# Attention heads in pairs at every second step, and the second mixer's gate factors one step earlier

## The chip, the cores and the metric

The kernel runs on one core of a Trainium2 chip. Its time is the device time of one execution in microseconds (us); the time of a kernel is the median of its runs. The engines of the core work side by side, each through its own queue in program order: TensorE (PE; weight loads are shown as PEld) multiplies and transposes, VectorE (DVE), ScalarE (ACT) and GpSimd (POOL) work on elements, and SyncE (SP) issues nearly all DMA transfers.

## The reference

One layer of a hybrid block for a sequence of 256 positions of width 1024, all in float32:

```python
ada = c @ w_ada + b_ada                       # shift, scale, gate
h = _rmsnorm(x, norm_w) * (1 + scale) + shift
(qa, ka, va, za, qm, km, vm, zm, om, ig, fg, ga, gm) = jnp.split(h @ w_in, SPLIT_IDX, axis=-1)
qa, ka = _rmsnorm(heads(qa)), _rmsnorm(heads(ka))
ya = merge(_moba_attention(qa, ka, heads(va), rel_bias))    # 8 heads of 128, causal, with a bias by distance
ya = (ya * silu(za)) @ w_att_proj
qm, km = jnp.split(silu(_causal_dwconv(concat(qm, km), conv_w, conv_b)), 2, axis=-1)
hm = _mlstm_chunkwise(qm, km * 256 ** -0.5, vm, ig + b_igate, fg + b_fgate)   # 4 heads of 256
ym = (rmsnorm(sigmoid(om) * hm) * silu(zm)) @ w_ml_proj
return x + gate * ((sigmoid(ga) * ya + sigmoid(gm) * ym) @ w_out)
```

With 256 positions there is a single block of attention, so the attention of one head is an ordinary causal softmax of 256 by 256. The second mixer (mLSTM) is computed here for the whole sequence at once, with factors made from the running sum and the running maximum of its two gates.

## The kernel before

**Precision.** Every large product is done in three matmuls: each float32 operand is split into a high part and a low part (ACT makes the high part `wh` of a weight tile, L448; DVE, or POOL for a few, the low part `wl`, L452), and high by high, low by high and high by low are summed in PSUM. The products of attention, scores and values, are plain float32 matmuls, which the trace shows as two records each. Transposes are matmuls against an identity.

**First stage.** The norm, the modulation and the products for q and k of attention run first, under a step list of their own (to about 55 us). The change doesn't touch it.

**The loop.** The rest is a list of chunks, each one half or one third of a weight matrix's columns: va (three chunks), za, qm, km, att (the projection after attention), zm, vm, om, ga, gm, ml and out (two chunks each). Each chunk is four steps `g`, and a step is the products with two blocks of 128 rows of the weight: 12 matmuls with 344 columns in the chunks of va (steps 0 to 11), 24 matmuls with 256 columns in za, qm, km and att (steps 12 to 43), 12 matmuls with 512 columns in zm, vm and om. `done(name, half)` is the first step after a chunk: 16 for the first half of za, 20 for its second.

**Order within a step.** In program order a step `g` (L950) does this: it splits the weights of step `g + 4` (`split`, L441): first `wh` on ACT, then the callbacks registered with `between(g, ...)`, then `wl` on DVE. When a chunk ends it takes its result out of PSUM. Then come the callbacks registered with `at(g, ...)`, then weight loads for buffers that came free (`pump`, L934, onto SP's queue), and last the step's own matmuls. Each engine executes its share in that order and waits where data are missing. Five buffers of `wh` and `wl` and six of raw weights are in use.

**Attention, by head `h`** (A0 is 10):

- `att_qk` (L599): two products give the scores, without the masked quarter, in one PSUM buffer `aux`; two DVE reductions add the bias, negate, and leave the row's extreme in `st`. P has 4 buffers.
- `att_exp` (L614): two exponents on ACT, with their sums. It is an `at` callback of step 10 + h.
- `att_norm` (L620): DVE takes the reciprocal of the sums and scales P, in two parts. At step 11 + h, ahead of the scores of the next head.
- `att_PT` (L626): three transposes of P on TensorE into one `aux` buffer, and a copy on ACT. At step 13 + h, ahead of all else that step has between.
- `att_av` (L634): for two heads, the product with the values (four matmuls), the product with silu(za) on DVE, and its split into `yah` (ACT) and `yal` (POOL). At steps 18, 20, 21 and 22 for heads 0, 2, 4 and 6 and the one after each.

`aux` (L431) is a ring of four PSUM buffers that all these share, the transposes of q and k (`qk_T`, at steps 7, 8, 10 and 12) and of the gates too.

**The second mixer's gates.** `gates_0` to `gates_7` (L518 on) work on a few rows of 256 values. `gates_4` (step 15) makes the running sum and maximum by DVE scans. `gates_5` (L561, step 17) takes the negative maximum and the sum of both on DVE, the exponent `GE` on ACT, and writes the negative maximum to memory (`md`, a DMA of SP). `gates_6` (step 18) reads it back spread over all partitions (`NM`, a DMA of SP). `gates_T` (L584, step 18) transposes `GE` on TensorE. `gates_7` (19) and `gates_D` (21) make the decay factors from NM.

Of the kernel before, what the change touches and what calls it, by code (L numbers as in the profile page):

```python
# [18 lines left out]
AH, AD = 8, 128  # L19
# [47 lines left out]
def tile_hybrid(ctx: ExitStack, tc: tile.TileContext, x, c, params2, w_row, w_va, ada_mod, ada_gate,  # L67
# [117 lines left out]
    def split_low(k, e, c0, c1):  # L185
        h, l = wsp[k]
        cs = slice(c0, c1)
        e.tensor_tensor(l[:, cs], wrow[k][:, cs], h[:, cs].bitcast(F32), op=OP.subtract)  # L188
# [44 lines left out]
    for j in range(4):  # L233
        n, q = divmod(j, 2)
# [68 lines left out]
    for step in P1_STEPS:  # L303
# [3 lines left out]
        else:  # L307
# [5 lines left out]
                 h=lambda k: split_low(k, nc.vector, 1536, NR), G=modulate_low,  # L313
# [35 lines left out]
    def done(name, half):  # L349
        return 4 * (C[name, half] + 1)  # L350
# [104 lines left out]
    hooks, hooks_between = {}, {}  # L455

    def at(step, fn, *a):
        hooks.setdefault(step, []).append((fn, a))

    def between(step, fn, *a):  # L460
        hooks_between.setdefault(step, []).append((fn, a))
# [45 lines left out]
    f = slice(32, 36)  # L507
# [375 lines left out]
    at(10, gates_2)  # L883
    at(12, qk_T, "k", 1)
    A0 = 10
    for h in range(AH):
        between(A0 + 1 + h, att_norm, h)
        between(A0 + h, att_qk, h)
        hooks_between.setdefault(A0 + 3 + h, []).insert(0, (att_PT, (h,)))
        at(A0 + h, att_exp, h)  # L890
    for step, fn in ((12, gates_3), (14, gates_copy), (15, gates_4), (17, gates_5), (18, gates_6), (18, gates_T),
                     (19, gates_7), (21, gates_D)):
        at(step, fn)
    for nm in ("qm", "km"):
# [3 lines left out]
                at(s + q, lambda i, *a: conv(mmt[i], *a), C[nm, hf], hf, nm, q)  # L898
                at(s + q + 1, conv_silu, hf, nm, q)
    for q in range(2):  # L900
        at(done("za", 0) + 2 + 2 * q, att_av, 2 * q)
        at(done("za", 1) + 1 + q, att_av, 4 + 2 * q)
    s = 4 * C["zm", 0]
    for half in range(2):
        at(s + 5 * half, ml_split, half)
# [170 lines left out]
```

## Time and profile before

| | |
|---|---|
| median of 3 runs | 351.48 us (351.43 to 351.65) |
| profiled execution, its own time | 351.84 us |
| its span, first to last instruction | 350.0 us |
| mean granted TensorE clock | 1.000 |
| PE busy | 344.3 us (98%) |
| DVE busy | 247.0 us (71%) |
| ACT busy | 213.3 us (61%) |
| POOL busy | 87.8 us (25%) |

Rows of a timeline give the start and the length of an instruction in us, the engine, the line in the kernel, the operation, what it writes and reads, shapes and a count; in brackets stands how long the engine was idle before it and what ended that. Matmuls are pipelined and their recorded ends are modelled, so their records overlap: what a matmul costs in a stream is the distance between two starts, not the length of its record. Rows of waits give who waited for whom, us in total, times, and the longest. Rows of stretches of time give the busy time of PE, PEld, DVE, ACT and POOL, each with its count, then the granted clock, the share of the DMA engines and GB/s.

### The profile page before, as it was taken

The page shows a single profiled execution, that of the slowest core. Times are in us where ns is not written, and L with a number is a line of the kernel's source. Part 1 is how long each engine was busy: PE and PEld are TensorE (multiplying, and loading weights), DVE is VectorE, ACT ScalarE, POOL GpSimd, SP SyncE. Part 2 cuts the span into 40 slices and gives each one's busy share as a digit, 9 for nine tenths or more (in the row PEclk, how much of TensorE's full clock was granted, in tenths as well). Part 3 has the DMA queues.
Part 4 walks back from the last instruction along what each step waited for, and adds up shares of the span by engine and source line. Part 5 has one row for each costly group of instructions (what it writes and reads, how often), then busy time and mean ns, then how long its engine had stood idle before and what let it go on. Part 6 is the DMA issues. An engine that isn't in the chain of part 4 may idle for free.

```text
span 350.0 us, 6175 instructions
## 1 busy us (share of the span) xinstructions
PE 344.3 (98%) x2432; PEld 323.1 (92%) x2432; DVE 247.0 (71%) x369; ACT 213.3 (61%) x331; POOL 87.8 (25%) x81
## 2 busy tenths in 40 slices
PE   8999999999999999999999999999999999999996
PEld 7788889999999999999998888888899999999995
DVE  4999996976994437768866693864475775469961
ACT  4768779799777867675646554445646374543510
POOL 4400002942202462555004352000010320452000
PEclk9999999999999999999999999999999999999999
DMA  7999999890671554493874837659119129291011
GB/s 286 416 413 416 415 419 418 223 385 13 197 285 62 161 200 134 151 375 125 322 279 151 330 120 245 237 163 388 51 29 381 72 70 367 107 292 69 2 62 60
DMA packets 23517, 77.79 MB, mean 222 GB/s; under 512 B 3001, under 2 KB 4929, under 8 KB 22849
## 3 DMA queue, kind: packets, MB, share of 16 engines
q1 hardware_dynamic: 23336, 76.87, 59.9%
q10 hardware_dynamic: 152, 0.53, 0.5%
q8 instruction: 19, 0.31, 0.3%
q14 instruction: 10, 0.07, 0.1%
HBM read 76.14 MB, written 1.25 MB: 221 GB/s over the span
## 4 chain that ended last, share of the span: by engine, by line
PE 96%; DMA 2%; DVE 1%; issue 0%; SPq 0%; ACT 0%; DVEq 0%; ACTq 0%
PE mm L1009 15%; PE mm L1006 15%; PE mm L1008 15%; PE pm L198 13%; PE mm L999 8%; PE mm L1000 8%; PE mm L1001 8%; PE mm L992 3%; DMA adat<-in_ada_mod_dram 2%; PE mm L1021 1%; PE aux L642 1%; PE mm L1020 1%; PE mm L1019 1%; PE aux L492 1%; PE aux L604 1%; PE aux L762 1%
## 5 line engine op out<-in xcount | busy, mean ns | idle before, releaser
L452 DVE TENSOR_TENSOR wl<-raw,wh 128x1024 fp32r<-128x1024 f32 (+1 forms) x92 | 118.7, 1302 | 64.1 <-ACT wh L448 64.1
L448 ACT CAST wh<-raw 128x1024 fp32r<-128x1024 f32 (+1 forms) x100 | 100.5, 1015 | 54.2 <-PE mm L1001 26.7
L1006 PE MATMUL mm<-hTh,wh 128*128 128x256 f32 x320 | 90.0, 281 | 0.0
L1008 PE MATMUL mm<-hTl,wh 128*128 128x256 f32 x320 | 88.7, 277 | 0.0
L1009 PE MATMUL mm<-hTh,wl 128*128 128x256 f32 x320 | 88.7, 277 | 0.0
L1006 PEld LDWEIGHTS mm<-hTh,wh 128*128 128x128 f32 x320 | 60.2, 188 | 0.0
L1008 PEld LDWEIGHTS mm<-hTl,wh 128*128 128x128 f32 x320 | 60.2, 188 | 0.0
L1009 PEld LDWEIGHTS mm<-hTh,wl 128*128 128x128 f32 x320 | 60.1, 188 | 0.0
L999 PE MATMUL mm<-wh,hTh 128*128 128x512 f32 (+1 forms) x144 | 53.0, 368 | 0.0
L1000 PE MATMUL mm<-wl,hTh 128*128 128x512 f32 (+1 forms) x144 | 52.6, 365 | 0.0
L1001 PE MATMUL mm<-wh,hTl 128*128 128x512 f32 (+1 forms) x144 | 52.6, 365 | 0.0
L1001 PEld LDWEIGHTS mm<-wh,hTl 128*128 128x128 f32 x144 | 27.0, 188 | 3.8
L999 PEld LDWEIGHTS mm<-wh,hTh 128*128 128x128 f32 x144 | 27.0, 188 | 3.6
L1000 PEld LDWEIGHTS mm<-wl,hTh 128*128 128x128 f32 x144 | 27.1, 188 | 3.5
L452 POOL TENSOR_TENSOR wl<-raw,wh 128x1024 fp32r<-128x1024 f32 x8 | 19.5, 2461 | 18.4 <-ACT wh L448 12.1
L183 ACT CAST wrh<-raw 128x512 fp32r<-128x512 f32 (+1 forms) x24 | 18.2, 761 | 8.0 <-DMA raw<-in_w_row_dram 7.9
L188 DVE TENSOR_TENSOR wrl<-raw,wrh 128x512 fp32r<-128x512 f32 (+1 forms) x26 | 20.3, 807 | 0.5 <-ACT wrh L183 0.5
L198 PE MATMUL pm<-wrh,hTh 128*128 128x512 f32 x64 | 19.9, 392 | 0.8 <-ACT hTh L168 0.8
L198 PE MATMUL pm<-wrh,hTl 128*128 128x512 f32 x64 | 19.8, 391 | 0.0
L198 PE MATMUL pm<-wrl,hTh 128*128 128x512 f32 x64 | 18.7, 391 | 0.0
L1009 PE MATMUL mm<-yah,wl 128*128 128x256 f32 x64 | 17.7, 276 | 0.0
L1006 PE MATMUL mm<-yah,wh 128*128 128x256 f32 x64 | 17.7, 276 | 0.0
(218 smaller groups left out, 659.3 us busy)
## 6 DMA issues: line engine op xcount, KB each, us to landing
raw<-in_w_in_dram SPq DMA_DIRECT2D x32, 1024.0 KB, 5.2
adat<-in_ada_mod_dram SPq DMA_DIRECT2D x16, 512.0 KB, 8.8
raw<-in_w_va_dram SPq DMA_DIRECT2D x6, 688.0 KB, 9.2
raw<-in_ada_gate_dram SPq DMA_DIRECT2D x4, 1024.0 KB, 6.8
raw<-in_w_att_proj_dram SPq DMA_DIRECT2D x4, 1024.0 KB, 4.8
raw<-in_w_ml_proj_dram SPq DMA_DIRECT2D x4, 1024.0 KB, 6.3
raw<-in_w_out_dram SPq DMA_DIRECT2D x4, 1024.0 KB, 6.3
raw<-in_w_row_dram SPq DMA_DIRECT2D x15, 256.0 KB, 8.1
```

Source lines behind the costliest of these rows:

```text
L183: copy(wsp[k][0][:, c0:c1], wrow[k][:, c0:c1])
L188: e.tensor_tensor(l[:, cs], wrow[k][:, cs], h[:, cs].bitcast(F32), op=OP.subtract)
L198: nc.tensor.matmul(pm[ch][:, t], a[:, k, t * 128:(t + 1) * 128], b[:, cs], start=k == 0 and i == 0, stop=k == KT - 1 and i == 2)
L448: nc.scalar.copy(h, w)
L452: e.tensor_tensor(l, w, h.bitcast(F32), op=OP.subtract)
L992: nc.tensor.matmul(mmt[ci][:, t, cs], a, w[:, kk, cs], start=first and i == 0 and c0 == 0 and w is wh, stop=last and i == 1 and c0 > 0, sk ...
L999: nc.tensor.matmul(o, a, wh[:, kk], start=first, stop=False)
L1000: nc.tensor.matmul(o, a, wl[:, kk], start=False, stop=False)
L1001: nc.tensor.matmul(o, b, wh[:, kk], start=False, stop=last)
L1006: nc.tensor.matmul(o, wh[:, kk, cs], sh_[:, k], start=first and i % 2 == 0, stop=False, skip_group_check=True)
L1008: nc.tensor.matmul(o, wh[:, kk, cs], sl_[:, k], start=False, stop=False, skip_group_check=True)
L1009: nc.tensor.matmul(o, wl[:, kk, cs], sh_[:, k], start=False, stop=last and i % 2 == 1, skip_group_check=True)
```

## The change

The callbacks of attention are registered for pairs of heads (h, h + 1) with h = 0, 2, 4, 6. Scores and exponents of both heads come at step 10 + h, the normalisation of both at step 11 + h, the transposes of both P at step 14 + h. So scores stand at steps 10, 12, 14 and 16, normalisation at 11, 13, 15 and 17, transposes at 14, 16, 18 and 20. Within a step the order is transposes, scores; the sort at the end of the new lines puts transposes first. The products with the values come for heads 0 to 3 at step 20 and for heads 4 to 7 at step 22. `gates_5` goes from step 17 to step 16. The functions that are called are not changed, nor is the number of their instructions.

```diff
     A0 = 10
-    for h in range(AH):
-        between(A0 + 1 + h, att_norm, h)
-        between(A0 + h, att_qk, h)
-        hooks_between.setdefault(A0 + 3 + h, []).insert(0, (att_PT, (h,)))
-        at(A0 + h, att_exp, h)
-    for step, fn in ((12, gates_3), (14, gates_copy), (15, gates_4), (17, gates_5), (18, gates_6), (18, gates_T),
+    for h in range(0, AH, 2):
+        for fn, d in ((att_PT, 4), (att_qk, 0), (att_norm, 1)):
+            for hh in (h, h + 1):
+                between(A0 + h + d, fn, hh)
+        for hh in (h, h + 1):
+            at(A0 + h, att_exp, hh)
+    for i in range(A0 + 4, A0 + AH + 4, 2):
+        hooks_between[i].sort(key=lambda f: f[0] is not att_PT)
+    for step, fn in ((12, gates_3), (14, gates_copy), (15, gates_4), (16, gates_5), (18, gates_6), (18, gates_T),
                      (19, gates_7), (21, gates_D)):
         at(step, fn)
...
     for q in range(2):
-        at(done("za", 0) + 2 + 2 * q, att_av, 2 * q)
-        at(done("za", 1) + 1 + q, att_av, 4 + 2 * q)
+        at(done("za", 1), att_av, 2 * q)
+        at(done("za", 1) + 2, att_av, 4 + 2 * q)
```

## The prediction

> **What bounds the kernel now.** I read the page first: the busy line and the chain of work that ended last, then who waited for whom on the matmul queue.
>
> ```profile
> PE 344.3 (98%) x2432; PEld 323.1 (92%) x2432; DVE 247.0 (71%) x369; ACT 213.3 (61%) x331; POOL 87.8 (25%) x81
> PE 96%; DMA 2%; DVE 1%; issue 0%; SPq 0%; ACT 0%; DVEq 0%; ACTq 0%
> PE pm L198 <- ACT hTh L168: 0.8, 1, 0.8
> ```
>
> TensorE is busy for 344.3 of 350.0 us and holds 96% of the chain; its last own wait of the whole run, 0.8 us, is in the first stage, at 11 us. So moving work of another engine gains nothing here by itself. Only three things can change the time: a TensorE wait inside the stage touched, TensorE's cost of going from one kind of matmul to another, and the pace of its stream. The stage is steps 10 to 22 of the loop, from about 76 us (L605 at 76.59 below) to 122.83. Its waits, weight loads included, hold one line for TensorE, and it is the gates':
>
> ```profile
> PEld aux L587 <- ACT GE L565: 0.2, 1, 0.2
> ```
>
> **Part 1, the gate factors one step sooner.** The timeline around step 18, DVE, ACT and PE:
>
> ```profile
> 101.81 0.16 DVE L622 RECIPROCAL st<-st 128x2 f32<-128x2 f32 x1
> 102.65 0.42 DVE L608 CUSTOM_DVE_ANT_0 P<-aux,Tb 128x256 f32<-128x256 f32 x1
> 103.21 1.22 DVE L452 TENSOR_TENSOR wl<-raw,wh 128x1024 fp32r<-128x1024 f32 x1
> 104.55 0.41 DVE L564 TENSOR_TENSOR G<-G 4x256 f32<-4x256 f32 x1
> 105.05 0.42 ACT L565 ACTIVATE GE<-G 4x256 f32<-4x256 f32 x1 [0.89 <-DVE st L622]
> 105.42 0.27 PE L631 MATMUL aux<-ident,P 128*128 128x128 f32 x1
> 105.62 0.31 PE L587 MATMUL aux<-ident,GE 36*128 36x36 f32 x2
> 105.86 0.70 PE L642 MATMUL aux<-PT,vat 128*128 128x256 f32 x2
> 106.40 0.38 PE L644 MATMUL aux<-PT,vat 128*128 128x128 f32 x2
> 106.62 0.60 PE L642 MATMUL aux<-PT,vat 128*128 128x256 f32 x2
> 107.05 0.38 PE L644 MATMUL aux<-PT,vat 128*128 128x128 f32 x2
> ```
>
> The GE factors are ready at 105.05 + 0.42 = 105.47; TensorE transposes them (L587) at 105.62. From the last transpose of P to it go 0.20 us where 0.11 is usual (94.00 to 94.33 for three, below), and the first L642 takes 0.54 to the next instruction where the second takes 0.43. That is 0.09 + 0.11 = 0.20 us, the size of the wait.
>
> With gates_5 at step 16, DVE no longer has ahead of it the normalisation of head 6 (101.81 to 102.65, at most 0.84) and the split for step 21 (1.22): about 2.0 us sooner, so GE is ready at about 103.5. On ACT the exponent of head 7 now stands before it, but its input is sooner too, since head 7 moves to step 16. TensorE asks at about 105.3, so the cover is some 1.8 us. **Gain 0.20**, bounds 0 (if DVE runs 1.8 us late) and 0.20. No new DVE, ACT or table load is issued. The step also issues a DMA, the write of md, and moves it past one step of SyncE's queue:
>
> ```profile
> 66.22 31.91 SPq L376 DMA_DIRECT2D raw<-in_w_in_dram  x8
> 104.65 0.32 SPq L567 DMA_DIRECT2D md<-G  x1
> 105.92 0.38 SPq L573 DMA_DIRECT2D NM<-md  x1
> 116.03 4.36 SPq L376 DMA_DIRECT2D raw<-in_w_in_dram  x2
> ```
>
> The eight weight loads before it are issued by 98.13 at the latest, from steps that lie before 16, and the next load comes at 116.03, after NM. Nothing is queued behind the waiting write but NM's read, which stays at step 18. Cost 0; if a load did stand behind it, it would lose the 2 us of earlier DVE work at most, against the lead shown in part 3.
>
> **Part 2, fewer changes between the two kinds of work.** Before, TensorE leaves its stream for attention at each of the steps 10 to 22: 13 blocks. After, scores come at 10, 12, 14 and 16, transposes of P at 14, 16, 18 and 20, values at 20 and 22, and the transposes of q, k and gates at 10, 12 and 18: 7 blocks. The matmuls in them are the same. So what a block costs beyond its matmuls counts six times:
>
> ```profile
> 76.59 0.38 PE L605 MATMUL aux<-kT,qT 128*128 128x128 f32 x2
> 76.81 1.04 PE L492 MATMUL aux<-ident,qt 128*128 128x128 f32 x8
> 94.00 0.27 PE L629 MATMUL aux<-ident,P 128*128 128x128 f32 x1
> 94.33 0.60 PE L604 MATMUL aux<-kT,qT 128*128 128x256 f32 x2
> 94.76 0.38 PE L605 MATMUL aux<-kT,qT 128*128 128x128 f32 x2
> 97.74 0.27 PE L629 MATMUL aux<-ident,P 128*128 128x128 f32 x1
> 110.02 0.27 PE L629 MATMUL aux<-ident,P 128*128 128x128 f32 x1
> 113.09 0.27 PE L629 MATMUL aux<-ident,P 128*128 128x128 f32 x1
> 122.83 0.36 PE L1006 MATMUL mm<-hTh,wh 128*128 128x256 f32 x1
> 182.77 0.40 PE L999 MATMUL mm<-wh,hTh 128*128 128x512 f32 x1
> ```
>
> The undisturbed stream is 22 steps of 24 matmuls from 122.83 to 182.77: 59.94 / 528 = 0.1135 us each, 2.72 a step. A step with a head takes 97.74 - 94.00 = 3.74. Taken off: 2.72, three transposes 0.33, L604 0.43, L605 0.22 (its distance to the next instruction inside a block, 76.59 to 76.81). What is left is 0.04; for transposes alone 3.07 - 2.72 - 0.33 = 0.02. I take 0.03 for steps 11, 13, 15 and 17 and 0.02 for 19 and 21: **gain 0.16**, bounds 0 and 0.24 (six times 0.04).
>
> **Part 3, what moves and stays hidden.** Scores of odd heads one step sooner, transposes of even heads one step later, values of heads 0 and 1 two steps later. The reduction that takes the scores waits for TensorE at the head of DVE's queue, and behind it stands the split of the weights four steps on. Its lead covers that:
>
> ```profile
> 108.78 1.22 DVE L452 TENSOR_TENSOR wl<-raw,wh 128x1024 fp32r<-128x1024 f32 x1 [3.16 <-ACT wh L448]
> ```
>
> This is the split for step 22, done at 110.00, used at 122.83: 12.8 us of lead, among the latest of the stage. A pair puts one head's reduction (102.65 to 103.21, 0.56) more ahead of it in an even step, and one head's normalisation (0.84) more in an odd one; on ACT one more exponent. All of it is under 3 us, so cost 0; without the lead it would be about a microsecond. The four score buffers in PSUM come round each two steps (7.5 us), the four P buffers too, and a buffer's transposes stand ahead of its next scores on TensorE. Values at 20 need transposed heads 0 to 3 copied at 14 and 16; their results are first used at step 36. Cost 0 each, nothing below 0 since TensorE waits for none of them today. The sort of the callbacks puts transposes first, where they already are.
>
> **Part 4, the pace, which the trace shows and does not explain.** Stretches between blocks run at one of two paces and mostly keep theirs to the next block. First and last rows of four stretches:
>
> ```profile
> 83.76 0.28 PE L1008 MATMUL mm<-hTl,wh 128*128 128x256 f32 x1
> 86.35 0.28 PE L1009 MATMUL mm<-hTh,wl 128*128 128x256 f32 x1
> 91.39 0.28 PE L1008 MATMUL mm<-hTl,wh 128*128 128x256 f32 x1
> 93.89 0.28 PE L1009 MATMUL mm<-hTh,wl 128*128 128x256 f32 x1
> 114.84 0.28 PE L1008 MATMUL mm<-hTl,wh 128*128 128x256 f32 x1
> 117.44 0.28 PE L1009 MATMUL mm<-hTh,wl 128*128 128x256 f32 x1
> 269.27 0.28 PE L1008 MATMUL mm<-hTl,wh 128*128 128x256 f32 x1
> 277.51 0.28 PE L1009 MATMUL mm<-hTh,wl 128*128 128x256 f32 x1
> ```
>
> 22 distances each in the first three: 0.1177, 0.1136, 0.1182; 70 in the fourth: 0.1177. A slow step costs 24 x 0.0042 = 0.10. Slow are steps 12 (first pair) and 20 (third), 13 by the same reading, and 10 and 11 with 12 matmuls each at half the price: 0.40 in the stage. Every block draws anew, the change alters every block, so this term is open: -0.40 if all turn quick, +0.70 if the seven others (14 to 19, 21) turn slow. I take 0, the same share as now, since nothing in the identical blocks says which pace follows (step 13 slow, step 14 quick, after the same instructions).
>
> **Sum.** -0.20 - 0.16 + 0 = -0.36. Against the profiled execution's own 351.84 (span 350.0 and 1.84 around it) that is 351.48; that execution lies 0.36 above the median of the runs, 351.48, and from the median the forecast is **351.12**. A measurement of this kernel tells a difference from about 0.2%, 0.70 us: below 350.78 or above 352.18. So I forecast no change that shows.
>
> **Rivals.**
>
> *The stream after step 22 goes slow.* The block that ends at 122.83 is followed by 528 matmuls with no further block. Now they are quick, after a block of one pair of heads; then it is a block of two pairs. If that stretch draws the slow pace and keeps it: 528 x 0.0042 = +2.2, 351.12 + 2.2 = 353.3. It shows as slower from 1.06 / 0.0042 = 252 slow matmuls on. For it: 72 matmuls at 269 us stayed slow throughout. Against: no stretch longer than those was slow. 0.08.
>
> *All short stretches turn quick.* 351.12 - 0.40 = 350.7. For it: steps 14 to 19 are almost all quick, and half as many draws. 0.20.
>
> *The short stretches turn slow instead,* half of the bound, +0.35 to +0.70: 351.5 to 351.8. For it: steps 10 to 13 are slow one after another. 0.12.
>
> *The earlier gates do nothing,* because DVE, which runs its stage without pause, gets to them late: 351.32. Against: 1.8 us of cover. 0.08.
>
> *The clock drops in the larger blocks.* If transposes and short matmuls of step 20 (two heads transposed 0.65, two pairs of values 2.6: 3.25 us) took twice their time on a lowered clock, and the next 24 matmuls too, that would be +3.25 and +2.72 at most; I take one step's, +2.7, so 353.8. The rows against it:
>
> ```profile
> L492 PE MATMUL aux<-ident,qt x8: 272/272/273, 76.8 to 77.6; 128*128 128x128 f32 x8
> 76.20:90.30 14.10, 14.10 (x109) 13.89 (x108) 10.27 (x26) 13.32 (x26) 5.24 (x6) 1.00 0.30 104
> ```
>
> Eight transposes in a row left the granted clock at 1.00 in that stretch. 0.02. The Trainium skill's TensorE: Matmul & The Clock Gate, Part 4: PE-mode transpose, states that the transpose mode does not count as busy work for the clock gate in the same way, at about 275 ns a transpose. By that rule grouping six transposes would speak against this change; the trace has the duration, 272 ns, but shows no lower clock behind them, and six are fewer than these eight.
>
> **Chances and range.** The forecast's own case 0.50, the rivals 0.20, 0.12, 0.08, 0.08 and 0.02. Faster by over 0.2% takes most of the quick rival and a little of the forecast, where later stretches (269 us, 0.30) turn quick as well: 0.22. Slower takes the long stretch, the clock and a little of the slow rival: 0.11. Within: 0.67. The range goes from 350.5 (both gains, all short stretches quick, some of the later ones) to 352.0 (no gain kept, most of the slow bound); the long stretch lies outside.
>
> **What would show it.** Right: no wait of L587 for GE, GE ready by 104 us; seven blocks, the stretches between them 48 matmuls long; step 22's block starting about 0.3 us sooner, but for the paces; TensorE with no new wait; the time from there to the end unchanged. Wrong: a wait of a matmul for wl, PT or an aux buffer between steps 14 and 24; a pace over 0.117 after step 22; a granted clock below 1.00.

## The result, and the profile after

The changed kernel is slower: 354.21 us median (353.84 to 354.51) against 351.46 us for the kernel before (351.32 to 351.65), a ratio of 1.0078 with a 95% interval of 1.0062 to 1.0094. The forecast was 351.12 us, 350.5 to 352.0, so the time lies outside the range. The rival that had 0.08, "the stream after step 22 goes slow" at 353.3 us, is what the trace shows.

In the kernel after, lines from L892 on stand three further down; the matmuls of the 256-column chunks are L1009, L1011 and L1012. In the kernels of the experiments that have lines added they stand further down still. The page of the kernel after, its busy line and its chain:

```profile
span 352.0 us, 6176 instructions
PE 346.6 (98%) x2432; PEld 325.1 (92%) x2432; DVE 246.8 (70%) x369; ACT 213.1 (61%) x331; POOL 90.6 (26%) x81
PE 97%; DMA 1%; ACT 0%; DVE 0%; SPq 0%; issue 0%
```

The span grew by 2.0 us, TensorE's busy time by 2.3, with the same 2432 matmuls. The other engines did no more than before, but for POOL's rough 2.8. So TensorE does the same work and takes longer, and the waits of the kernel after say that it doesn't wait for it:

```profile
PE warm L227 <- POOL ident masks.py:199: 1.4, 1, 1.4
PE xps L263 <- ACT diag L246: 0.8, 1, 0.8
PEld aux L587 <- issue: 0.2, 1, 0.2
```

The first two lie in the first stage. The third is the old 0.2 us ahead of the gates' transposes, with another name in the place of GE. The time is in the distances between matmuls. TensorE's timeline of the kernel after (start, length, line), the first and second rows of stretches and the last ones:

```profile
69.20 0.40 PE L1002 MATMUL mm<-wh,hTh 128*128 128x344 f32 x1
...
98.95 0.28 PE L1011 MATMUL mm<-hTl,wh 128*128 128x256 f32 x1
...
104.18 0.28 PE L1012 MATMUL mm<-hTh,wl 128*128 128x256 f32 x1
...
104.84 0.27 PE L631 MATMUL aux<-ident,P 128*128 128x128 f32 x1
105.05 0.31 PE L587 MATMUL aux<-ident,GE 36*128 36x36 f32 x2
...
105.51 0.29 PE L1011 MATMUL mm<-hTl,wh 128*128 128x256 f32 x1
...
110.94 0.29 PE L1012 MATMUL mm<-hTh,wl 128*128 128x256 f32 x1
...
122.53 0.36 PE L1009 MATMUL mm<-hTh,wh 128*128 128x256 f32 x1
122.73 0.28 PE L1011 MATMUL mm<-hTl,wh 128*128 128x256 f32 x1
...
184.69 0.28 PE L1012 MATMUL mm<-yah,wl 128*128 128x256 f32 x1
184.80 0.39 PE L1002 MATMUL mm<-wh,hTh 128*128 128x512 f32 x1
...
192.99 0.49 PE L757 MATMUL aux<-qmT,kmT 128*128 128x128 f32 x3
```

And two rows of the same view of the kernel before, which the sums below need:

```profile
69.52 0.40 PE L999 MATMUL mm<-wh,hTh 128*128 128x344 f32 x1
...
190.96 0.60 PE L757 MATMUL aux<-qmT,kmT 128*128 128x128 f32 x4
```

Read by differences. A stretch of 48 matmuls has 46 distances from its second to its last: steps 16 and 17 go at (104.18 - 98.95) / 46 = 0.1137 us, steps 18 and 19 at (110.94 - 105.51) / 46 = 0.1180, and steps 20 and 21, read in the same way, at 0.1180. The long stretch of 528 goes at (184.69 - 122.73) / 526 = 0.1178; before it went at 0.1134 by the same reading. From its start to the first matmul with 512 columns it takes 184.80 - 122.53 = 62.27 us, before 182.77 - 122.83 = 59.94: **2.33 us more**. What lies around it hardly moves: from step 7 to its start 53.33 us (before 122.83 - 69.52 = 53.31), and from its end to L757 8.19 us in both. So nearly the whole 2.0 us of the span is this one stretch, less the 0.3 us by which it starts sooner. The medians differ by 2.75, since the profiled execution of the kernel after was the lowest of its four and that of the kernel before above its median.

The groups of TensorE's weight loads in that stretch show a second mark of the slow pace (before from 122.83 to 182.7 us, then after from 122.53 to 184.7 us; count, busy us, mean ns):

```profile
L1006 PEld LDWEIGHTS mm<-hTh,wh 128*128 128x128 f32 x112 | 21.0, 188 | 0.0
L1008 PEld LDWEIGHTS mm<-hTl,wh 128*128 128x128 f32 x112 | 21.0, 188 | 0.0
L1009 PEld LDWEIGHTS mm<-hTh,wl 128*128 128x128 f32 x112 | 21.0, 188 | 0.0
```

```profile
L1012 PEld LDWEIGHTS mm<-hTh,wl 128*128 128x128 f32 x112 | 21.5, 192 | 0.0
L1011 PEld LDWEIGHTS mm<-hTl,wh 128*128 128x128 f32 x112 | 21.0, 188 | 0.0
L1009 PEld LDWEIGHTS mm<-hTh,wh 128*128 128x128 f32 x112 | 21.0, 188 | 0.0
```

In the slow stretch one of the three lines, here L1012, has weight loads of 192 ns, the others keep 188. In the thirteen traces of this study, 181 stretches with 256 columns follow a block. Among the first 24 matmuls of each, all of the 58 slow ones have such a line, which of the three differs, and none of the 123 quick ones has it. Cut into pieces of 24 to their ends, all stretches together give 222 slow pieces with the mark, 609 quick ones without it, and one in which the pace changes.

### The profile page after: what moved, and what is told of

Same layout as the page of the kernel before. It is cut to its first block, busy times and chain, and to the rows that moved or that the text cites. A ratio compares the mean times of both kernels' runs of the same rounds, so it can differ in the third digit from the quotient of the medians.

```text
span 352.0 us, 6176 instructions
## 1 busy us (share of the span) xinstructions
PE 346.6 (98%) x2432; PEld 325.1 (92%) x2432; DVE 246.8 (70%) x369; ACT 213.1 (61%) x331; POOL 90.6 (26%) x81
## 4 chain that ended last, share of the span: by engine, by line
PE 97%; DMA 1%; ACT 0%; DVE 0%; SPq 0%; issue 0%
PE mm L1009 15%; PE mm L1011 15%; PE mm L1012 15%; PE pm L198 13%; PE mm L1002 8%; PE mm L1003 8%; PE mm L1004 8%; PE mm L995 3%; DMA xt<-in_x_dram 1%; PE xps L263 1%; PE mm L1024 1%; PE mm L1023 1%; PE mm L1022 1%; PE aux L492 1%; PE aux L642 1%; PE aux L604 1%
## 5 line engine op out<-in xcount | busy, mean ns | idle before, releaser
L1009 PE MATMUL mm<-hTh,wh 128*128 128x256 f32 x320 | 90.2, 282 | 0.0
L1011 PE MATMUL mm<-hTl,wh 128*128 128x256 f32 x320 | 89.3, 279 | 0.0
L1012 PE MATMUL mm<-hTh,wl 128*128 128x256 f32 x320 | 89.3, 279 | 0.0
L1012 PEld LDWEIGHTS mm<-hTh,wl 128*128 128x128 f32 x320 | 60.6, 189 | 0.0
L1009 PEld LDWEIGHTS mm<-hTh,wh 128*128 128x128 f32 x320 | 60.3, 189 | 0.1
L1011 PEld LDWEIGHTS mm<-hTl,wh 128*128 128x128 f32 x320 | 60.1, 188 | 0.0
L1012 PE MATMUL mm<-yah,wl 128*128 128x256 f32 x64 | 18.0, 281 | 0.0
L1009 PE MATMUL mm<-yah,wh 128*128 128x256 f32 x64 | 18.0, 281 | 0.0
```

The source lines that it names most:

```text
L1009: nc.tensor.matmul(o, wh[:, kk, cs], sh_[:, k], start=first and i % 2 == 0, stop=False, skip_group_check=True)
L1011: nc.tensor.matmul(o, wh[:, kk, cs], sl_[:, k], start=False, stop=False, skip_group_check=True)
L1012: nc.tensor.matmul(o, wl[:, kk, cs], sh_[:, k], start=False, stop=last and i % 2 == 1, skip_group_check=True)
```

## The experiments

Each was timed beside the kernel before on the same chip: that had 351.31 us in the first two groups and 351.36 in the last. Pace means the distance between starts in the long stretch, from its second to its last matmul. The ratio is estimated from the single runs and is not the quotient of the two medians.

### The parts alone

**Pairs and gates without the moved values:**

```diff
-        at(done("za", 1), att_av, 2 * q)
-        at(done("za", 1) + 2, att_av, 4 + 2 * q)
+        at(done("za", 0) + 2 + 2 * q, att_av, 2 * q)
+        at(done("za", 1) + 1 + q, att_av, 4 + 2 * q)
```

> The changed kernel with the values left as before (two heads each at steps 18, 20, 21 and 22); pairs and earlier gates stay. Theory A (the larger block of values at step 22 leaves TensorE at the slow pace): the stretch after step 22 is back at 0.1134 us a matmul, time 350.8 to 351.4. Theory B (the pace is drawn by the whole state that any block leaves, whatever its size): either 350.8 to 351.4 or 353.0 to 353.7, nothing between. Theory C (the earlier gates, and with them the transfers and GpSimd work beside the stretch, slow TensorE): slow, 353 or more.

**Only the values moved, on the kernel before:** the same lines the other way round.

> The kernel before with only the values moved (heads 0 to 3 at step 20, 4 to 7 at step 22). Theory A: slow stretch, 351.46 + 2.2 - 0.04 = 353.6 (353.2 to 354.2). Theory B: that, or 351.2 to 351.7. Theory C: no change, 351.3 to 351.7.

**Only the gates, on the kernel before:**

```diff
-    ... (15, gates_4), (17, gates_5), (18, gates_6), ...
+    ... (15, gates_4), (16, gates_5), (18, gates_6), ...
```

> The kernel before with only the gate factors one step sooner. My price was 0.20 us less, 351.26. Theory A: 351.1 to 351.4, the stretch after step 22 quick. Theory B: that, or about 353.5. Theory C: about 353.5 or more. In all of them the wait of the gates' transposes for GE (0.2 us) is gone.

**The last calls apart,** so that the block of step 22 holds one pair, as before the change:

```diff
-        at(done("za", 1) + 2, att_av, 4 + 2 * q)
+        at(done("za", 1) + 1 + q, att_av, 4 + 2 * q)
```

> The changed kernel with the last two calls for the values apart: heads 0 to 3 at step 20, 4 and 5 at step 21, 6 and 7 alone at step 22, so that the last block before the long stretch is the one of the kernel before. Theory A: 350.9 to 351.5, quick. Theory B: either 350.9 to 351.5 or 353.0 to 354.2. Theory C: slow, 353 or more.

| kernel | median us | ratio (95%) | long stretch, us | pace |
|---|---|---|---|---|
| pairs and gates | 351.11 | 1.0002 (0.9989 to 1.0015) | 123.90 to 183.84 | 0.1134 |
| values only | 353.87 | 1.0076 (1.0060 to 1.0093) | 122.70 to 184.97 | 0.1178 |
| gates only | 351.48 | 1.0000 (0.9991 to 1.0009) | 122.76 to 182.71 | 0.1134 |
| last calls apart | 351.29 | 1.0002 (0.9993 to 1.0012) | 122.33 to 182.28 | 0.1134 |

The moved values alone bring the whole loss; the pairs and the gates bring neither gain nor loss that can be told from none. The timeline of the values-only kernel, the end of step 18's block and the ends of the long stretch:

```profile
105.21 0.31 PE L587 MATMUL aux<-ident,GE 36*128 36x36 f32 x2
105.45 0.39 PE L1006 MATMUL mm<-hTh,wh 128*128 128x256 f32 x1
...
122.90 0.28 PE L1008 MATMUL mm<-hTl,wh 128*128 128x256 f32 x1
...
184.85 0.28 PE L1009 MATMUL mm<-yah,wl 128*128 128x256 f32 x1
```

Its pace is (184.85 - 122.90) / 526 = 0.1178. Its block at step 18 now ends with the gates' transposes, since the values that used to follow them have gone, and the stretch behind it is slow already, at 0.118, four steps ahead of step 22's block.

The gates-only kernel decides on part 1 of the prediction. Its timeline, ACT and TensorE:

```profile
102.46 0.42 ACT L565 ACTIVATE GE<-G 4x256 f32<-4x256 f32 x1 [0.89 <-DVE st L622]
...
105.36 0.27 PE L631 MATMUL aux<-ident,P 128*128 128x128 f32 x1
105.56 0.31 PE L587 MATMUL aux<-ident,GE 36*128 36x36 f32 x2
105.80 0.70 PE L642 MATMUL aux<-PT,vat 128*128 128x256 f32 x2
106.33 0.38 PE L644 MATMUL aux<-PT,vat 128*128 128x128 f32 x2
```

GE is ready at 102.88, 2.68 us ahead of L587. The 0.20 us from L631 to L587 and the 0.53 of the first L642 are, to 0.01, what they were when GE came at 105.47. So they are not a wait for GE. They stay with the small transposes: in every trace of this case 0.20 to 0.21 us go from the matmul ahead of L587 to it, also where the gates' transposes come first in their block, behind a matmul of the stream.

### Is it the size of the last block, or what came before it?

Theory C, by which the earlier gates slow TensorE, is out: three kernels above have the earlier gates and a quick long stretch. Theory B allowed either pace in each kernel, so these runs can't tell against it. Of theory A two forms were left: four heads together at step 22 make the stream slow, or the block hands on the pace that it finds. The first kernel keeps that block and moves only heads 2 and 3; the second only puts the gates' transposes ahead of those of P, so that step 18's block ends otherwise.

```diff
-        at(done("za", 1), att_av, 2 * q)
+        at(done("za", 1) + q, att_av, 2 * q)
```

> The changed kernel with the first two calls for the values apart (heads 0 and 1 at step 20, 2 and 3 at step 21); heads 4 to 7 stay together at step 22. Theory Z (a block of values for four heads at step 22 gives the slow pace whatever stands before): slow after step 22, 353.2 to 354.2. Theory S (the pace is handed on from stretch to stretch: it turns slow at step 18, where the gates' transposes are now the last thing in the block; a block of values for two heads turns slow into quick, as at step 21 of the kernel before, and one for four heads leaves it as it is): step 21 quick, after step 22 quick, 351.0 to 351.5. Theory B (drawn anew by each block): either.

```diff
-    ... (18, gates_6), (18, gates_T),
+    ... (18, gates_6),
...
+    hooks_between[18].insert(0, (gates_T, ()))
     for i in range(A0 + 4, A0 + AH + 4, 2):
-        hooks_between[i].sort(key=lambda f: f[0] is not att_PT)
+        hooks_between[i].sort(key=lambda f: f[0] not in (att_PT, gates_T))
```

> The changed kernel with the transposes of the gates ahead of those of P in step 18, so that the block there ends with full transposes. The values for four heads stay at steps 20 and 22. Theory Z: step 22 slow, 353.2 to 354.2. Theory S: steps 18 to 21 quick (0.113 after the first few matmuls) and after step 22 quick, 350.7 to 351.2. Theory B: either.

The first gave 351.35 us (0.9998, 0.9987 to 1.0008) with the long stretch quick behind the same block of four heads, at (182.15 - 122.53) / 526 = 0.1133:

```profile
122.53 0.28 PE L1011 MATMUL mm<-hTl,wh 128*128 128x256 f32 x1
...
182.15 0.28 PE L1012 MATMUL mm<-yah,wl 128*128 128x256 f32 x1
```

So the size of the last block alone isn't the cause. The second gave 353.54 us (1.0061, 1.0045 to 1.0078), against its forecast of quick. Its timeline shows that half of that forecast held:

```profile
105.19 0.29 PE L1012 MATMUL mm<-hTl,wh 128*128 128x256 f32 x1
...
110.44 0.28 PE L1013 MATMUL mm<-hTh,wl 128*128 128x256 f32 x1
...
113.95 0.28 PE L1012 MATMUL mm<-hTl,wh 128*128 128x256 f32 x1
...
119.37 0.28 PE L1013 MATMUL mm<-hTh,wl 128*128 128x256 f32 x1
...
122.23 0.28 PE L1012 MATMUL mm<-hTl,wh 128*128 128x256 f32 x1
...
184.18 0.28 PE L1013 MATMUL mm<-yah,wl 128*128 128x256 f32 x1
```

Behind step 18 the stream is quick now, (110.44 - 105.19) / 46 = 0.1141 with a few slow distances at its start. But behind the block of step 20, six transposes and four heads, it is slow, (119.37 - 113.95) / 46 = 0.1178, and behind step 22's as well, (184.18 - 122.23) / 526 = 0.1178. So the changed kernel goes slow at step 18, and without that it goes slow at step 20.

### One block more

One transpose of the identity into a buffer that nobody reads, as a block of its own at step 23, in the changed kernel and in the kernel before:

```diff
+    def kick(n):
+        pa = aux([128, 512])
+        for i in range(n):
+            nc.tensor.transpose(pa[:, i * 128:(i + 1) * 128], ident, ident)
+
+    at(23, kick, 1)
```

> The changed kernel with one transpose of the identity more, into a buffer that nothing reads, ahead of the matmuls of step 23, in the middle of the slow stretch; its price is about 0.13 us. Theory Z and theory B with luck: the stretch is quick from step 23 on, 354.0 - 2.1 + 0.1 = 352.0 (351.4 to 352.2 with the session's 351.3 for the kernel before). If one transpose leaves the pace (theory S allows both, since no such block stands in the traces): 353.6 to 354.6. If the pace had to do with the traffic of other engines or with addresses, the transpose could not change it: 353.6 to 354.6 too.

> The kernel before with the same single transpose ahead of step 23, in the middle of its quick stretch. If only large blocks or states handed on give the slow pace (theories Z and S): quick, 351.3 + 0.13 = 351.4 (351.1 to 351.8). Theory B: that, or slow from step 23 on, 351.3 + 2.1 + 0.1 = 353.5.

The changed kernel with it took 355.30 us (1.0113, 1.0097 to 1.0129), above every time that was forecast for it; the kernel before took 351.45 (1.0003, 0.9990 to 1.0017), as forecast. The transpose left the pace as it was, slow in the one (0.1178) and quick in the other (0.1134). But in the changed kernel it altered a stretch 158 us later. Its timeline there:

```profile
283.05 0.28 PE L1017 MATMUL mm<-hTl,wh 128*128 128x256 f32 x1
...
327.93 0.28 PE L1017 MATMUL mm<-yml,wh 128*128 128x256 f32 x1
...
328.16 0.28 PE L1001 MATMUL mm<-wh,yh 128*128 128x256 f32 x1
...
336.73 0.28 PE L1001 MATMUL mm<-wl,yh 128*128 128x256 f32 x1
...
340.47 0.28 PE L1028 MATMUL mm<-wh,yh 128*128 128x256 f32 x1
```

That is 381 distances, (327.93 - 283.05) / 381 = 0.1178, where the kernels before and after go at 0.1133: 1.7 us more. No block ends this slow pace: at 328.16 the last chunk begins, whose matmuls come in another order (L1001), some fifteen matmuls later the stream is quick, and it stays so, (340.47 - 336.73) / 33 = 0.1133. Two stretches ahead of it changed as well, one of 24 to slow and one of 72 to quick. They lie behind blocks of four equal transposes, which so leave either pace.

From the traces up to here I had a rule for the blocks ahead of the long stretch: one pair's values leave the stream quick, four heads' values or a transpose leave it at the pace that they find. It was put to three more kernels: the values of heads 6 and 7 computed once more at step 23, unread; heads 0 and 1 back at step 18 and 2 and 3 at 20, with 4 to 7 together at 22; and the transpose of the identity at the end of step 22's block.

```diff
+    def again(h0):
+        ...
+            nc.tensor.matmul(pa[:, hh, :], T["va"][:, 0, h * 128:(h + 1) * 128], T["PT"][:, h, 0:256], start=hh == 0,
+        ...
+    at(23, again, 6)
```

> The changed kernel with one block more: at step 23, before the matmuls of that step, the four matmuls with the values of heads 6 and 7 are done once more into a buffer of PSUM that nobody reads (some 1.3 us of TensorE more, by 0.43 + 0.22 for each head). Theory of handing on (what follows a block depends on the pace before it and on the kind of block; one pair of heads has turned a slow stretch quick in both kernels that show it): the step of 24 matmuls before it stays slow, the 504 after it are quick, 354.2 + 1.3 - 504 x 0.0044 = 353.3. Theory of chance by a few ns (the kind of block says nothing): either pace, and if slow 354.2 + 1.3 = 355.5; later stretches may change too, by up to 2.1 in the last long one of 480.

```diff
-        at(done("za", 1), att_av, 2 * q)
+        at(done("za", 1) - 2 + 2 * q, att_av, 2 * q)
```

> The changed kernel with the values of heads 0 and 1 at step 18, of 2 and 3 at step 20, and of 4 to 7 together at 22 as in the change. Its last block of attention is that of the changed kernel, and its stretch of 48 matmuls before it follows a block of six transposes and one pair. Theory of handing on: one pair at 20 leaves a quick stretch, four heads from quick leave quick, so the long stretch is quick, 351.1 to 351.4. Theory that four heads together at 22 make it slow whatever comes before (already against one run): 353.5. Theory of chance: either.

```diff
+    at(22, kick, 1)
```

> The changed kernel with one transpose of the identity into a buffer that nobody reads, at the end of the block of step 22, right ahead of the long stretch: 0.11 us more in a block that stands anyway. Theory of handing on by the kind of block: transposes have left a slow stretch slow, so 354.2 + 0.1 = 354.3. Theory of chance by a few ns: the pace is drawn anew, so the long stretch can be quick, 352.0, and later stretches can change as well (plus or minus up to 2.1).

| kernel | forecast by the rule, us | measured us | ratio (95%) | pace |
|---|---|---|---|---|
| values once more at 23 | 353.3 | 352.94 | 1.0043 (1.0028 to 1.0058) | 0.1133 |
| two pairs, then four heads | 351.1 to 351.4 | 350.96 | 0.9987 (0.9976 to 0.9998) | 0.1133 |
| transpose at the end of 22 | 354.3 | 353.71 | 1.0074 (1.0058 to 1.0090) | 0.1178 |

In all three the long stretch has the pace that the rule said; the times lie 0.1 to 0.6 us below the forecasts. The timeline of the first, from its new block on:

```profile
126.45 0.59 PE L910 MATMUL aux<-PT,vat 128*128 128x256 f32 x2
...
127.68 0.37 PE L1019 MATMUL mm<-hTh,wh 128*128 128x256 f32 x1
127.89 0.28 PE L1021 MATMUL mm<-hTl,wh 128*128 128x256 f32 x1
...
184.78 0.28 PE L1022 MATMUL mm<-yah,wl 128*128 128x256 f32 x1
```

1.23 us of unread matmuls (126.45 to 127.68) turn a slow stream quick and win back more than they cost: (184.78 - 127.89) / 502 = 0.1133. The second kernel's median is 0.40 us under that of the kernel before, a ratio whose interval just stays below 1, at the limit of what can be told here.

The rule, counted over all blocks between 104 and 128 us in the thirteen traces whose kind comes three times or more. Kernels that share their blocks up to some point agree there, so these are not all independent cases:

| block | from slow | from quick |
|---|---|---|
| ends with the gates' transposes | none | slow 7 |
| gates' transposes, then one pair's values | none | quick 5 |
| one pair's values alone | quick 5 | quick 7 |
| four heads' values alone | slow 5 | quick 2 |
| six transposes, then four heads | slow 5 | slow 1 |
| six transposes, then one pair | quick 1 | quick 2 |
| three transposes, then one pair | none | slow 3 |
| three transposes alone | slow 1 | quick 3 |

## Why the prediction was wrong

**The step that failed** is part 4: "Every block draws anew", and with it "I take 0": the term held the stage alone, and the 528 matmuls behind it, whose block the change altered too, were left to a rival outside the range. They cost 2.33 us. Behind blocks of values the pace is not drawn: in the kernel before the long stretch follows one pair's values, which left the stream quick in all 12 cases of the table, and in the changed kernel four heads' values, which left it as they found it in all 7. It had turned slow at step 18, behind the gates' transposes. For other blocks the prediction's reason stands: those of steps 13 and 14 issue the same matmuls, each behind a slow stretch, and in all four traces that have them the first leaves it slow and the second quick. The prediction's reason for a chance of 0.08, that no stretch longer than 72 was slow, counted the two long stretches of the trace, 528 and 576 matmuls, as if their length spoke. In the trace of before, 72 matmuls keep the slow pace to their end, and of the 17 stretches with 256 columns behind a block 5 are slow throughout; from that a chance of 0.3 would have followed, and a range that reached 353.3. The price was right: 528 x 0.0042 = 2.2 forecast, 2.33 measured.

**The short stretches** of part 4, taken as 0, gave about that: steps 12 and 13 turned quick (-0.20), 18, 19 and 21 slow (+0.30), 20 stayed slow, a sum of +0.10 at the prediction's 0.10 a step.

**Part 1, gain 0.20 by the earlier gates,** was worth 0. GE came sooner, at 104.30 here (before 105.47), though not at the 103.5 of the prediction nor by its sign of 104; with the gates alone it was 102.88. L587 followed L631 by 0.20 to 0.21 all the same. The row of ACT in the kernel after:

```profile
103.88 0.42 ACT L565 ACTIVATE GE<-G 4x256 f32<-4x256 f32 x1 [0.57 <-DVE st L622]
```

The row of waits had named GE because it came last, not because TensorE lost time by it. The prediction's bound of 0 and its fourth rival stood for this, with another reason.

**Part 2, gain 0.16 by six fewer blocks.** The seven blocks came as said, and from step 12 on the stretches of 48. The stage from step 7 to the long stretch is 0.02 longer; with +0.10 from the paces that leaves -0.08 for blocks and gates. In the kernel with two pairs and then four heads, whose steps 12, 13 and 20 are quick, it is 122.02 - 69.09 = 52.93, 0.38 shorter than before, of which 0.30 are paces, and again 0.08 is left. So by this reckoning the gain was about half of what was forecast, within its bounds of 0 and 0.24. The two rows of that kernel's timeline:

```profile
69.09 0.40 PE L1002 MATMUL mm<-wh,hTh 128*128 128x344 f32 x1
...
122.02 0.37 PE L1009 MATMUL mm<-hTh,wh 128*128 128x256 f32 x1
```

**Part 3, moves that stay hidden,** held: no wait of TensorE was added.

**The clock** did not drop. The stretches of the kernel after, from step 7 to the long stretch and the long stretch (PE, PEld, DVE, ACT, POOL, granted clock, DMA share, GB/s):

```profile
69.20:122.50 53.30, 53.30 (x416) 52.24 (x414) 37.15 (x83) 44.35 (x88) 15.63 (x15) 1.00 0.52 190
122.53:184.60 62.07, 62.07 (x530) 62.07 (x529) 42.99 (x72) 37.67 (x51) 22.03 (x10) 1.00 0.60 222
```

The slow pace comes at a granted clock of 1.00. The Trainium skill's TensorE: Matmul & The Clock Gate, Part 4: PE-mode transpose, would have let blocks rich in transposes weigh on the clock; six of them ahead of four heads' values show nothing of that here, with 1.00 in the first of these rows.

**What stays open** is why a block leaves the pace that it leaves. The granted clock is 1.00 in both paces, TensorE waits for nobody, and the kernels with quick and slow stretches issue the same matmuls there. Blocks of four equal transposes near 270 us leave either pace, as those of steps 13 and 14 do, so the kind of block alone doesn't decide. Nor is a block needed: 24 matmuls with 256 columns that stand directly behind ones with 512 (from 255.00 us in the kernel before) go at 0.1178 in all thirteen traces. The moment at which the matmuls meet the weight loads may decide. That isn't shown.

## What to carry to other kernels

Where TensorE is never idle, look at the distances between its matmuls before counting what a change of order saves: two paces 4% apart, 0.1133 and 0.1178 us, were worth six times the gain that was looked for. Ask of each long stretch which block goes ahead of it, price it at both paces, and let the range hold both. And a wait that the trace gives to the last input to come is a stall only if it goes when the input comes sooner; a kernel with that one edit settles it.

## What was not expected of the hardware

A stream of matmuls with 256 columns has two paces at the same granted clock, 0.1133 and 0.1178 us a matmul, and can keep the slow one for 528 matmuls, 62 us; in one kernel it left it without a block, where the order of the matmuls changed. The slow one goes with weight loads of 192 in place of 188 ns on one of three lines. It is the program that settles it and not the single execution: the four timed runs of the changed kernel lie within 0.7 us, all above the highest of the kernel before beside them. A single transpose 158 us earlier changed the pace of a stretch, and 1.23 us of unread matmuls, in the right place, brought the changed kernel's median from 354.21 to 352.94 us (the kernel before beside them had 351.46 and 351.36).
